# A hybrid decoder layer: three projections in products of 512 columns, and background steps handed out at another pace

## The chip, the cores and the metric

The kernel runs on one core of a Trainium2 chip. The metric is the device time of one execution in microseconds (us), lower is better; the median of three runs stands for the kernel. Beside it there is one profiled execution, whose trace gives every instruction of the engines: TensorE (PE for matmuls, PEld for weight loads), VectorE (DVE), ScalarE (ACT), GpSimd (POOL) and SyncE (SP), and the packets of the DMA queues.

## The reference

One decoder layer over 256 tokens of width 1024, in float32: a SwiGLU feed-forward (FFN), then a mixer of two parallel branches, then a second FFN, each between norms. Only the mixer's first projection and what reads it concern us:

```python
u = rmsnorm(h, mix_pre_g[l])
z, xbc, dt_raw, q, k, v, gate_logits = jnp.split(u @ w_in[l], IN_SPLITS, axis=-1)
y_ssd = ssd_branch(z, xbc, dt_raw, ...)     # chunked state-space scan; y * silu(z), norm, @ w_branch
y_att = diff_attn_branch(q, k, v, ...)      # 8 heads, two softmaxes each, p0 - lam * p1, norm, @ w_branch
gates = jax.nn.sigmoid(gate_logits + gate_b[l]).reshape(b, L, N_BRANCH, D_MODEL)
merged = gates[:, :, 0] * y_ssd + gates[:, :, 1] * y_att
h = h + rmsnorm(merged @ w_out[l], mix_post_g[l])
```

z has 2048 columns, q and k have 1024 each; q is scaled by 1/8 before the scores.

## The kernel before

**Precision and products.** Every float32 matrix is split into a high and a low part in a reduced float format (`F32R`): `hi` is a cast, `lo` is the rest. A product is the sum of three: high weight by high activation, high weight by low activation, low weight by high activation. Activations `u` live in two tiles in which, for each slab of 128 input channels, the 256 high columns and the 256 low columns lie next to each other. `act_u` (L430) hands out the high part, the low part, or both at once as 512 columns.

**Weights.** Weights come by DMA in chunks of 1 MB (`raw`, three buffers, on SP's queue), and each chunk is split into two `whi` tiles by ACT (L249) and two `wlo` tiles by DVE (L252). `take()` (L276) returns the next chunk's parts and first splits as many chunks as three ahead. These tiles are from a pool of 29 buffers of 4 KB a partition (`k4`), which also holds most tiles of the mixer.

**Two ways to make a product of 256 output channels by 256 tokens.** `mm_t` (L293) makes it with 256-column matmuls: for each half of 128 channels 8 slabs by (high weight x high activation, high weight x low activation), then 8 slabs of low weight x high activation, so 48 matmuls, each with its weight load; the high weight is loaded twice. Both halves share one PSUM bank, and one ACT operation moves it to SBUF. `mm_w` (L305) loads the high weight once and multiplies it with both activations in a matmul of 512 columns, and the low weight with the high activation in one of 256: 32 matmuls and weight loads. Each half fills a whole PSUM bank, with the sum in the first 256 columns and the high x low term in the other 256. ACT copies the second part to the destination (L318) and DVE adds the first part to it (L319). Both take banks from a pool of three, `pj` (L79). Before the change `mm_w` serves the FFNs alone, and `mm_t` serves B and C, xs, z, q and k.

**The order of the mixer.** After v come products for B and C, eight for xs (each followed by the causal convolution on DVE), eight for z (L1321 to L1327), then silu on z, four times q and k (L1333 to L1345), then the gates as four `natural` products of 512 channels (L1352, L1384: two weight chunks and two blocks of 128 tokens each, 12 matmuls of 512 columns at a time), then the SSD branch product `pws`, the attention branch product `pwd`, and the output product.

**The background.** Work that is no large product is written as generators and woven in between the products. A generator does a step and yields its declared cost in us. `back.run(us)` (L1293) adds credit and takes steps until the credit is spent; an overshoot is carried as debt, and a step that yields `BREAK` ends the call and keeps what credit is left. The steps, in the order of the queue:

- `ssd_work`, for each of four groups: two steps that transpose xs and multiply it with dt (0.6 each), four blocks E of exponentials (1.4 each), one state product `py` and its sums on DVE (1.6): 8.4 a group. A group also issues two row broadcasts `acb` by DMA on POOL's queue.
- `ssd_norm`, added after z, for each group: xs * silu(z) and its square (1.2), sums and split (1.5), `BREAK`, a matmul `pn` and the inverse root (0.1), the scaling and split into `yh`, `yl` (2.8); two groups are under way at a time.
- `att_work`, added after q and k, for pairs of heads: scores and softmax (2.3 a head), the combination of the two softmaxes (1.3 a head) with the transposes of the pair before, `BREAK`, values and norm (1.8), transpose of the output (0.8).

A call follows each z, q and k product with `BG_US`, each of the 16 gate blocks with `GATE_US`, and each of the 16 `pws` blocks with `SSD_US`.

**Who sets the order.** From the end of the first v products up to line 1350 the framework's planner orders the instructions of every engine by the place in the program and its own estimate of when they are ready. From line 1350, `own_order(PE)`, PE runs its matmuls in the order in which they are written, while the planner goes on ordering the other engines. Every engine executes its list strictly in order.

Of the kernel before, what the change touches and what calls it, by code (L numbers as in the profile page):

```python
# [18 lines left out]
AF = mybir.ActivationFunctionType  # L19
ALU = mybir.AluOpType  # L20
# [7 lines left out]
T = 256  # L28
# [12 lines left out]
WARM = 3  # L41
FILL = 2
TAIL = 3
BG_US = 3.15
GATE_US = 1.35
SSD_US = 1.55
DOWN = {"f1": "p q1 p p q2 p ppp", "f2": "q1 p q2 p q3 ppp"}
FIRST, LAST = (1, 2, 3, 5, 7, 6, 4), (1, 6, 7, 2, 5, 3, 4)
# [4 lines left out]
def tile_hybrid_layer(ctx: ExitStack, tc: tile.TileContext, x, ffn1_pre_g, ffn1_w_gate, ffn1_w_up,  # L53
# [4 lines left out]
    nc = tc.nc  # L58
# [5 lines left out]
    def k4(shape, name, dt=F32):  # L64
        return sb.tile(shape, dt, tag="k4", name=name, bufs=K4_BUFS)
# [13 lines left out]
    def pj(name):  # L79

        return ps.tile([P, 512], F32, tag="pj", name=name, bufs=3)

    def pjt(name):

        return pj(name).rearrange("p (m t) -> p m t", m=2)

    def bg(shape, name):
        return ps.tile(shape, F32, tag="bg", name=name, bufs=5)
# [169 lines left out]
    def split_to(n):  # L258

        while len(splits) < min(n, len(units)):  # L260
            of, p = units[len(splits)]
            if p is not None:
                splits.append(of.split(p))
                continue
            for _ in split_steps():
                pass

    def ahead_of(i, n):

        n *= 4  # L270
        while n > 0 and i < len(units):
            n -= 4 if units[i][1] is None else 1
            i += 1
        return i

    def take(ahead=AHEAD):  # L276

        i = taken[0]
        taken[0] += 1
        split_to(ahead_of(i, ahead))  # L280
        (of, p), w = units[i], splits[i]
        splits[i] = None
        if p is not None:
            return w
        his, los = w
        nj = chunks[of][1][1] // 2
        return (lambda j: his[j // nj][:, j % nj, :], lambda j: los[j // nj][:, j % nj, :])
# [5 lines left out]
    def mm_t(acc, w, act, k0=0, first=True, last=True, ks=range(KD)):  # L293

        (wh, wl), (ah, al, _) = w, act
        acc = acc if isinstance(acc, list) else [acc[:, m, :] for m in range(2)]
        for m in range(2):
            cs = slice(m * P, (m + 1) * P)
            for j in ks:
                nc.tensor.matmul(acc[m], wh(j)[:, cs], ah(k0 + j), start=first and j == ks[0], stop=False)  # L300
                nc.tensor.matmul(acc[m], wh(j)[:, cs], al(k0 + j), start=False, stop=False)  # L301
            for j in ks:
                nc.tensor.matmul(acc[m], wl(j)[:, cs], ah(k0 + j), start=False, stop=last and j == ks[-1])  # L303

    def mm_w(dst, name, w, act):  # L305


        (wh, wl), (ah, _, ahl) = w, act
        for m in range(2):
            acc = pj(f"{name}{m}")  # L310
            cs = slice(m * P, (m + 1) * P)
            for j in range(KD):
                if j:
                    nc.tensor.matmul(acc[:, :T], wl(j)[:, cs], ah(j), start=False, stop=False)  # L314
                nc.tensor.matmul(acc, wh(j)[:, cs], ahl(j), start=j == 0, stop=j == KD - 1)  # L315
                if not j:
                    nc.tensor.matmul(acc[:, :T], wl(j)[:, cs], ah(j), start=False, stop=False)
            nc.scalar.copy(dst[:, m, :], acc[:, T:])  # L318
            nc.vector.tensor_tensor(dst[:, m, :], acc[:, :T], dst[:, m, :], ALU.add)  # L319

    def mm_nat(acc, w, act, k0, first, last, late):

# [26 lines left out]
    def act_table(name):  # L349
        f = nc.scalar.preload_act_table_set(name)  # L350
        for prev in act_since:
            tc.add_manual_dep(f.ins, prev, order, reason="activation table")
        act_since.clear()
        act_fence[0] = f.ins.name
# [71 lines left out]
    def new_u(tag):  # L426
        for i in range(2):
            uT[i] = sb.tile([P, 4, 2, T], F32R, tag="u8", name=f"u{i}_{tag}", bufs=2)

    act_u = (lambda j: uT[j // 4][:, j % 4, 0, :], lambda j: uT[j // 4][:, j % 4, 1, :],  # L430
             lambda j: uT[j // 4][:, j % 4, :, :])
# [294 lines left out]
    def ffn(post_v, tag, ready, turned, then, products):  # L726
# [28 lines left out]
        for j in range(2, FF // T):  # L755
            if j % 2 == 0:
                gh = k4([P, 4, T], f"gh_{tag}{j}", F32R)
                gl = k4([P, 4, T], f"gl_{tag}{j}", F32R)
            o = (j % 2) * 2
            gu += [(gh[:, o + m, :], gl[:, o + m, :]) for m in range(2)]  # L760
            sg = k2([P, 2, T], f"sg_{tag}{j}")
            mm_w(sg, f"pg_{tag}{j}", take(), act_u)
            act(sg, sg, AF.Silu)
            su = k2([P, 2, T], f"su_{tag}{j}")
            mm_w(su, f"pup_{tag}{j}", take(), act_u)
            nc.vector.tensor_tensor(sg, su, sg, ALU.mult)  # L766
            split(gh[:, o:o + 2, :], gl[:, o:o + 2, :], sg)
            if j // 2 in QUADS[tag]:
                if j % 2:
                    sums[j // 2] = sums_of(j // 2, even, sg)  # L770
                else:
                    even = sg
# [253 lines left out]
    for i in range(4):  # L1026
        acc = pjt(f"pbc{i}")
        mm_t(acc, take(), act_u)
        dst = (bT, cT)[i // 2]
# [16 lines left out]
    sz = [None] * 4  # L1046
# [94 lines left out]
    qT = [None] * 2  # L1141
    kT = [None] * 2
# [167 lines left out]
    back = Background()  # L1310
    back.add(cb_work())
    for g in range(4):
        xs[g] = k4([P, 4, T], f"xs{g}")
        for i in range(2):
            acc = pjt(f"pxs{g}{i}")
# [5 lines left out]
    for g in range(4):  # L1321
        sz[g] = k4([P, 4, T], f"sz{g}")
        for i in range(2):
            acc = pjt(f"pz{g}{i}")
            mm_t(acc, take(), act_u)
            nc.scalar.copy(sz[g][:, i * 2:i * 2 + 2, :], acc)
            back.run(BG_US)  # L1327
    act_table(SILU)
    for g in range(4):
# [3 lines left out]
    for c in range(4):  # L1333
        if c % 2 == 0:
            qT[c // 2] = k4([P, 4, T], f"q{c}")
            kT[c // 2] = k4([P, 4, T], f"k{c}")
        o = (c % 2) * 2
        acc = pjt(f"pq{c}")
        mm_t(acc, take(), act_u)
        nc.scalar.activation(qT[c // 2][:, o:o + 2, :], acc, AF.Copy, scale=0.125)  # L1340
        back.run(BG_US)
        acc = pjt(f"pk{c}")
        mm_t(acc, take(), act_u)
        nc.scalar.copy(kT[c // 2][:, o:o + 2, :], acc)
        back.run(BG_US)  # L1345

    back.add(att_work())

# [3 lines left out]
    def natural(name, n, hi, lo, evict, us, then=lambda: None):  # L1352


        accs = [pj(f"{name}{b}") for b in range(2)]
        for i in range(n):
            w = take()
            for b in range(2):
                bs = slice(b * P, (b + 1) * P)
                mm_nat(accs[b], w, (lambda k: hi(k)[:, bs], lambda k: lo(k)[:, bs]), i * 4, i == 0, i == n - 1, "u")  # L1360
                if i == n - 1:
                    evict(b, accs[b])
                back.run(us)
            if i == 0:
                then()
# [9 lines left out]
    for half in range(2):  # L1375
# [4 lines left out]
        for q in range(2):  # L1380
            def gate(b, acc):
                nc.vector.tensor_tensor(gt[half][b][:, halves[q]], acc, gb[:, halves[q]], ALU.add)

            natural(f"pgt{half}{q}", 2, uh, ul, gate, GATE_US)  # L1384
    opens.append(open_gates)
# [42 lines left out]
    acc = [[bg([P, 512], f"acc_mx{b}{q}") for q in range(2)] for b in range(2)]  # L1428
# [47 lines left out]
```

## Time and profile before

| what | us |
|---|---|
| median of three runs (739.06 to 739.86) | 739.17 |
| the profiled execution | 739.06 |
| its span, first to last instruction | 737.4 |

A row such as `L319 DVE TENSOR_TENSOR su_f<-pup_f,su_f 128x256 ... x36 | 15.1, 421 | 26.1 <-ACT` reads: line 319, on DVE, writes tile `su_f` from `pup_f` and `su_f`, on 128 partitions by 256 elements, 36 times; 15.1 us busy, 421 ns each on average; the engine was idle 26.1 us just before them, most of it until an ACT instruction. Buffer numbers are left out of tile names. A row of the timeline gives start, length, engine, line and tiles, with a number of like instructions merged; starts are in us from the beginning of the span. A row of waits reads: who waited, for what, us in total, times, longest. In the rows by stretch each engine has its busy time and in brackets its instructions. A matmul's busy time includes its latency through the array, so successive matmuls overlap, and their pitch is read from starts.

### The profile page before, as it was taken

To read this page: it belongs to the slowest core of one execution; us is meant where nothing else is said; L and a number is where in the kernel's file an instruction comes from. 1 tells how busy PE (TensorE), PEld (TensorE's weight loads), DVE (VectorE), ACT (ScalarE), POOL (GpSimd) and SP (SyncE) were. 2 spreads that over 40 slices of the span, in tenths; PEclk is the share of its full clock that TensorE was granted. 3 is DMA by queue.
4 is the path that set the end of the run, shared out by engine and by line. 5 is a ranking of instruction groups with operands and counts; after the bars stand their busy time and mean duration, and the time that the engine had idled before them with its cause. 6 is when DMAs were issued, how large, how long until landed. Compare 5 with 4: busy or idle time off the path is not lost.

```text
span 737.4 us, 11114 instructions
## 1 busy us (share of the span) xinstructions
PE 728.1 (99%) x4339; PEld 635.0 (86%) x4339; DVE 586.8 (80%) x888; ACT 460.6 (62%) x769; POOL 38.9 (5%) x72
## 2 busy tenths in 40 slices
PE   8999999999999999999999999999999999999996
PEld 6888888888889999999999888888888888888874
DVE  7978768998677888777878997685784878779994
ACT  6657556665566565959957666782563657566562
POOL 2700000000300000000000000000010000000000
PEclk9999999999999999999999999999999999999999
DMA  8884674469353647666556555365371764664541
GB/s 298 228 262 151 216 229 171 160 214 344 117 172 117 207 137 231 195 184 221 169 162 214 171 172 208 134 234 194 120 237 44 229 195 155 222 215 142 189 168 57
DMA packets 94214, 137.97 MB, mean 187 GB/s; under 512 B 2685, under 2 KB 68305, under 8 KB 94161
## 3 DMA queue, kind: packets, MB, share of 16 engines
q1 hardware_dynamic: 91488, 129.51, 53.7%
q0 software_dynamic: 2368, 7.22, 3.2%
q8 instruction: 34, 0.56, 0.3%
q10 hardware_dynamic: 304, 0.53, 0.2%
q14 instruction: 20, 0.16, 0.1%
HBM read 136.17 MB, written 1.08 MB: 186 GB/s over the span
## 4 chain that ended last, share of the span: by engine, by line
PE 96%; DVE 2%; issue 1%; ACT 0%; DMA 0%; DVEq 0%; ACTq 0%
PE pup_f L315 9%; PE pg_f L315 9%; PE pws L330 6%; PE pgt L330 6%; PE acc_f1p L620 5%; PE pg_f L314 4%; PE pup_f L314 4%; PE acc_f2p L620 3%; PE pn_f L330 3%; PE pn_f L340 3%; PE acc_mx L568 3%; PE pn_mx L330 3%; PE pwd L330 3%; PE acc_f1p L568 3%; PE pz L301 2%; PE pxs L303 2%
## 5 line engine op out<-in xcount | busy, mean ns | idle before, releaser
L252 DVE TENSOR_TENSOR wlo<-raw,whi 128x1024 fp32r<-128x1024 f32 (+1 forms) x226 | 266.5, 1209 | 25.3 <-ACT whi L249 22.2
L249 ACT CAST whi<-raw 128x1024 fp32r<-128x1024 f32 (+1 forms) x225 | 225.8, 1043 | 21.2 <-PE pgt L330 5.9
L315 PE MATMUL pg_f<-u_f,whi 128*128 128x512 f32 x288 | 101.3, 396 | 0.0
L315 PE MATMUL pup_f<-u_f,whi 128*128 128x512 f32 x288 | 101.3, 396 | 0.0
L314 PE MATMUL pg_f<-u_f,wlo 128*128 128x256 f32 x252 | 70.6, 280 | 0.0
L314 PE MATMUL pup_f<-u_f,wlo 128*128 128x256 f32 x252 | 70.2, 279 | 0.0
L315 PEld LDWEIGHTS pup_f<-u_f,whi 128*128 128x128 f32 x288 | 52.8, 188 | 9.9 <-issue 0.2
L315 PEld LDWEIGHTS pg_f<-u_f,whi 128*128 128x128 f32 x288 | 52.8, 188 | 9.7
L314 PEld LDWEIGHTS pg_f<-u_f,wlo 128*128 128x128 f32 x252 | 47.5, 188 | 1.7
L314 PEld LDWEIGHTS pup_f<-u_f,wlo 128*128 128x128 f32 x252 | 47.5, 188 | 1.7
L319 DVE TENSOR_TENSOR su_f<-pup_f,su_f 128x256 f32<-128x256 f32 x36 | 15.1, 421 | 26.1 <-ACT su_f L318 26.0
L129 ACT CAST wqh<-wt 128x1024 fp32r<-128x1024 f32 x20 | 21.1, 1053 | 23.5 <-DVE wt L121 17.2
L318 ACT COPY su_f<-pup_f 128x256 f32<-128x256 f32 x36 | 13.4, 372 | 35.1 <-PE pup_f L315 35.0
L330 PE MATMUL pgt<-whi,u_mx 128*128 128x512 f32 x128 | 33.1, 393 | 0.0
L300 PE MATMUL pxs<-u_mx,whi 128*128 128x256 f32 x128 | 31.7, 285 | 0.0
L301 PE MATMUL pz<-u_mx,whi 128*128 128x256 f32 x128 | 31.6, 284 | 0.0
L300 PE MATMUL pz<-u_mx,whi 128*128 128x256 f32 x128 | 31.6, 284 | 0.0
L301 PE MATMUL pxs<-u_mx,whi 128*128 128x256 f32 x128 | 31.4, 283 | 0.0
L330 PEld LDWEIGHTS pgt<-whi,u_mx 128*128 128x128 f32 x128 | 23.6, 188 | 5.4 <-DVE yl L291 0.3
L1004 DVE SCALAR_TENSOR_TENSOR xs<-pxs,cols_b,xs 128x255 f32<-128x255 f32 (+2 forms) x48 | 21.9, 476 | 6.3 <-ACT xs L1001 5.9
L290 ACT CAST gh_f<-sg_f 128x512 fp32r<-128x512 f32 x18 | 11.2, 621 | 21.8 <-DVE sg_f L766 21.8
L301 PEld LDWEIGHTS pz<-u_mx,whi 128*128 128x128 f32 x128 | 24.5, 192 | 0.2 <-issue 0.2
(395 smaller groups left out, 1709.5 us busy)
## 6 DMA issues: line engine op xcount, KB each, us to landing
raw<-in_w_in_dram SPq DMA_DIRECT2D x40, 1024.0 KB, 5.4
raw<-in_ffn_w_down_dram SPq DMA_DIRECT2D x22, 1024.0 KB, 4.9
raw<-in_ffn_w_gate_dram SPq DMA_DIRECT2D x20, 1024.0 KB, 5.6
raw<-in_ffn_w_up_dram SPq DMA_DIRECT2D x20, 1024.0 KB, 5.5
raw<-in_ssd_w_branch_dram SPq DMA_DIRECT2D x8, 1024.0 KB, 5.1
acb<-acd POOLq DMA_DIRECT2D x8, 512.0 KB, 5.2
raw<-in_da_w_branch_dram SPq DMA_DIRECT2D x4, 1024.0 KB, 5.1
raw<-in_w_out_dram SPq DMA_DIRECT2D x4, 1024.0 KB, 5.0
```

What stands on the lines that cost most here:

```text
L129: nc.scalar.copy(hi, src)
L249: copy(hi[:, js, :], r[:, q * nj + j:q * nj + j + n, :])
L252: nc.vector.tensor_sub(lo[:, js, :], r[:, q * nj + j:q * nj + j + n, :], hi[:, js, :].bitcast(F32))
L300: nc.tensor.matmul(acc[m], wh(j)[:, cs], ah(k0 + j), start=first and j == ks[0], stop=False)
L301: nc.tensor.matmul(acc[m], wh(j)[:, cs], al(k0 + j), start=False, stop=False)
L314: nc.tensor.matmul(acc[:, :T], wl(j)[:, cs], ah(j), start=False, stop=False)
L315: nc.tensor.matmul(acc, wh(j)[:, cs], ahl(j), start=j == 0, stop=j == KD - 1)
L330: nc.tensor.matmul(acc, a(k0 + j), b(j), start=first and i == 0, stop=last and i == 11)
L340: nc.tensor.matmul(accs[b], x_(k0 + j), w_(j), start=first and j == 0 and w_ is wh and x_ is acts[b][0], stop=last and j == 3 and w_ is wl)
L568: nc.tensor.matmul(acc[b][q], x_[:, ts], w_(kt)[:, halves[q]], start=begin and i == 0 and kt == 0 and x_ is ah and w_ is wh, stop=i == n - ...
L620: nc.tensor.matmul(bank[p], x_, w_, start=p not in begun, stop=last and p in (1, 5, 6, 7))
L1004: nc.vector.scalar_tensor_tensor(dst[:, m, s:], acc[:, m, :T - s], cw(3 - s, c), dst[:, m, s:], ALU.mult, ALU.add)
```

## The change

z, q and k go through `mm_w` instead of `mm_t`. `mm_w` gets a `scale`, used by q, which is applied by ACT to the second part and by DVE to the first. The paces are new: `BG_US`, now of z alone, 2.7 instead of 3.15; `QK_US` 2.8 after q and k, where 3.15 was used; `GATE_US` 1.75 instead of 1.35. `SSD_US` stays at 1.55.

```diff
-BG_US = 3.15
-GATE_US = 1.35
+BG_US = 2.7
+QK_US = 2.8
+GATE_US = 1.75
 SSD_US = 1.55
...
-    def mm_w(dst, name, w, act):
+    def mm_w(dst, name, w, act, scale=None):
...
-            nc.scalar.copy(dst[:, m, :], acc[:, T:])
-            nc.vector.tensor_tensor(dst[:, m, :], acc[:, :T], dst[:, m, :], ALU.add)
+            if scale is None:
+                nc.scalar.copy(dst[:, m, :], acc[:, T:])
+                nc.vector.tensor_tensor(dst[:, m, :], acc[:, :T], dst[:, m, :], ALU.add)
+            else:
+                nc.scalar.activation(dst[:, m, :], acc[:, T:], AF.Copy, scale=scale)
+                nc.vector.scalar_tensor_tensor(dst[:, m, :], acc[:, :T], scale, dst[:, m, :], ALU.mult, ALU.add)
...
-            acc = pjt(f"pz{g}{i}")
-            mm_t(acc, take(), act_u)
-            nc.scalar.copy(sz[g][:, i * 2:i * 2 + 2, :], acc)
+            mm_w(sz[g][:, i * 2:i * 2 + 2, :], f"pz{g}{i}", take(), act_u)
             back.run(BG_US)
...
-        acc = pjt(f"pq{c}")
-        mm_t(acc, take(), act_u)
-        nc.scalar.activation(qT[c // 2][:, o:o + 2, :], acc, AF.Copy, scale=0.125)
-        back.run(BG_US)
-        acc = pjt(f"pk{c}")
-        mm_t(acc, take(), act_u)
-        nc.scalar.copy(kT[c // 2][:, o:o + 2, :], acc)
-        back.run(BG_US)
+        mm_w(qT[c // 2][:, o:o + 2, :], f"pq{c}", take(), act_u, 0.125)
+        back.run(QK_US)
+        mm_w(kT[c // 2][:, o:o + 2, :], f"pk{c}", take(), act_u)
+        back.run(QK_US)
```

## The prediction

> **What bounds the kernel now.** I read the page first: busy times, the chain that ended last, the costliest groups.
>
> ```profile
> span 737.4 us, 11114 instructions
> PE 728.1 (99%) x4339; PEld 635.0 (86%) x4339; DVE 586.8 (80%) x888; ACT 460.6 (62%) x769; POOL 38.9 (5%) x72
> PE 96%; DVE 2%; issue 1%; ACT 0%; DMA 0%; DVEq 0%; ACTq 0%
> L319 DVE TENSOR_TENSOR su_f<-pup_f,su_f 128x256 f32<-128x256 f32 x36 | 15.1, 421 | 26.1 <-ACT su_f L318 26.0
> L318 ACT COPY su_f<-pup_f 128x256 f32<-128x256 f32 x36 | 13.4, 372 | 35.1 <-PE pup_f L315 35.0
> ```
>
> PE carries 96% of the chain. A busy PE may still be a waiting PE, so the list of PE's waits comes second; it is complete in four rows.
>
> ```profile
> PE warm L406 <- POOL ident L392: 1.6, 1, 1.6
> PE pn_f L340 <- DVE raw_u L459: 0.3, 1, 0.3
> PE pu_f L451 <- DMA h<-in_x_dram: 0.2, 1, 0.2
> PE acc_f2p L568 <- DVE wlo L252: 0.2, 1, 0.2
> ```
>
> None of them lies in the mixer. So in z, q/k and gates the kernel is as long as the stream of matmuls, and only two things can move the end: fewer PE nanoseconds, or another engine becoming late. Third, the stretches: z (289.4 to 344.0), q/k (to 397.2), gates (to 447.2), the SSD branch product (to 502.5), the busiest part of the gates, and all of z to gates together.
>
> ```profile
> 289.40:344.00 54.60, 54.58 (x475) 52.74 (x474) 42.85 (x73) 40.23 (x82) 2.65 (x5) 1.00 0.65 203
> 344.00:397.20 53.20, 53.20 (x462) 51.44 (x461) 42.90 (x62) 41.56 (x68) 1.59 (x3) 1.00 0.57 173
> 397.20:447.20 50.00, 50.00 (x249) 40.86 (x248) 43.86 (x76) 30.64 (x61) 0.53 (x1) 1.00 0.64 214
> 447.20:502.50 55.30, 55.30 (x298) 45.94 (x296) 44.82 (x75) 42.53 (x80) 0.00 (x0) 1.00 0.54 191
> 402.20:442.80 40.60, 40.60 (x200) 32.85 (x199) 36.89 (x67) 24.50 (x52) 0.53 (x1) 1.00 0.55 178
> 289.40:447.20 157.80, 157.78 (x1181) 145.04 (x1180) 129.61 (x209) 112.43 (x209) 4.78 (x9) 1.00 0.62 196
> ```
>
> After the length the columns are PE, PEld, DVE, ACT, POOL, granted clock, DMA. VectorE is the second engine: 82% over z to gates (129.61 of 157.80), 91% for 40 us of the gates, and PE did not wait even there.
>
> **The products (what is removed).** The first matmuls of consecutive products give their pitch. The first three rows are the FFN, which already has the 512-column form; the last two are the first z product, which no background work interrupts.
>
> ```profile
> 42.92 0.39 PE L315 MATMUL pg_f<-u_f,whi 128*128 128x512 f32 x1
> 48.52 0.39 PE L315 MATMUL pup_f<-u_f,whi 128*128 128x512 f32 x1
> 54.11 0.39 PE L315 MATMUL pg_f<-u_f,whi 128*128 128x512 f32 x1
> 289.50 0.28 PE L300 MATMUL pz<-u_mx,whi 128*128 128x256 f32 x1
> 295.26 0.38 PE L1056 MATMUL px<-ident,xs 128*128 128x128 f32 x2
> ```
>
> New form: (54.11 - 42.92) / 2 = 5.595 us. Old form: 295.26 - 289.50 = 5.76 us. Both push the same 12,288 columns; 48 matmuls and weight loads become 32. Gain 0.165 us a product, and 16 products (8 z, 4 q, 4 k): 2.6 us. It lies on the path whole, since PE never waits there. The Trainium skill (TensorE: Matmul & The Clock Gate, "Back-to-back issue gap") counts columns / 2.4 plus 2.5 ns a matmul; that would give 16 x 16 x 2.5 ns = 0.64 us, an estimate from that page and a time of 738.4. The two pitches above show four times that, 0.165 against 0.04 us a product, and they decide.
>
> **The evictions (what is added).** Before, one ACT operation moved both halves of a product:
>
> ```profile
> L1326 ACT COPY sz<-pz x8: 560/586/590, 295.5 to 344.3; 128x512 f32<-128x512 f32 x8
> ```
>
> Now each half has an ACT copy of 128x256 (0.372 us, row L318) and a DVE add that reads PSUM (0.421 us, row L319). ACT: 32 x 0.372 - 16 x 0.586 = 2.5 us more, against 45 us in which it is idle from z to gates: nothing. DVE: 32 x 0.42 = 13.4 us more. The four q products scale in the add, a form this trace lacks for a PSUM operand of that kind; the nearest row is the scaled sum below, 0.476, so 0.42 to 0.48 and at most 0.5 us more in all; I take 0.42, since the read of PSUM is that of L319.
>
> **The pace (what is moved).** Each paced step has a declared cost and a call hands out steps until its credit is spent. Credit to the end of the gates is unchanged: 16 x 3.15 + 16 x 1.35 = 72.0 before, 8 x 2.7 + 8 x 2.8 + 16 x 1.75 = 72.0 after. From there on all lies where it did, save that the first pair's values and norm slip one call, past the gates. Spending the credits by hand: the last E block and the state product of SSD group 2 move from z to q/k; three norm steps of groups 2 and 3 (square, sums, square) move from q/k to the gates; in the gates the attention starts at the seventh call instead of the fifth.
>
> ```profile
> L1078 DVE TENSOR_TENSOR E<-E,cbm 128x768 f32<-128x768 f32 x16 | 15.3, 957 | 7.9 <-ACT E L357 7.9
> L1073 DVE TENSOR_SCALAR E<-acb,acs 128x128 f32<-128x128 f32 x32 | 7.1, 280 | 0.0
> L1095 DVE SCALAR_TENSOR_TENSOR xs<-xs,cols_b,py 128x256 f32<-128x256 f32 x16 | 6.9, 476 | 1.9 <-PE py L1088 1.9
> L1102 DVE TENSOR_TENSOR xs<-xs,sz 128x1024 f32<-128x1024 f32 x4 | 4.8, 1221 | 1.4 <-ACT sz L357 1.4
> L1106 DVE TENSOR_TENSOR sqy<-sqy 128x512 f32<-128x512 f32 x4 | 2.7, 683 | 0.0
> L1107 DVE TENSOR_TENSOR sqy<-sqy 128x256 f32<-128x256 f32 x4 | 1.7, 423 | 0.1
> L291 DVE TENSOR_TENSOR ssum<-sqy,ssum 128x256 fp32r<-128x256 f32 x4 | 1.7, 417 | 0.0
> 289.40:447.20 157.80, 11.28 (x128) 8.01 (x128) 1.00 0.62 196
> acb<-acd POOLq DMA_DIRECT2D x8, 512.0 KB, 5.2
> ```
>
> An E block is (15.3 + 7.1) / 16 = 1.4 us of DVE, a state product's sums 6.9 / 4 = 1.7, and its matmuls 11.28 / 4 = 2.8 us of PE (row before the last: L1088 alone). Three norm steps are 2 x 1.22 + 0.68 + 0.42 + 0.42 = 4.0 us of DVE. The attention pair takes 1.3 us of PE (447.2 less its start at 445.96, quoted below) out of the gates. VectorE's load by stage then:
>
> z: 42.85 + 6.7 - 3.1 = 46.5 in 54.6 - 1.3 - 2.8 = 50.5 us, 92%.
> q/k: 42.90 + 6.7 + 3.1 - 4.0 = 48.7 in 53.2 - 1.3 + 2.8 = 54.7 us, 89%.
> Gates: 43.86 + 4.0 = 47.9 in 50.0 - 1.3 = 48.7 us, 98%.
> Together 143.0 in 153.9, 93%, so it still fits, narrowly; the branch product behind it has 55.3 - 44.8 = 10.5 us free on DVE, into which lag can run off.
>
> No load of weights is issued elsewhere. The moved steps bring no DMA but the row-sum broadcasts of SSD group 3 on POOL's queue, whose engine is 5% busy; they start later together with the E blocks that need them, so I cost them at nothing; if one landed late, its E block would be late by a landing, 5.2 us in the fence above, and the group's state product behind it. Norm tiles of groups 2 and 3 stay three calls longer (a call is 50.0 / 16 = 3.1 us) in the shared pool of 4 KB tiles, so the gates' weight splits find fewer free ones. That is not in the sum; it belongs to the slower rival.
>
> **The wait that is new.** The DVE add waits for its ACT copy; queued behind it on DVE are weight low parts and background steps, and PE waits for the add through PSUM: three banks, now one a half product instead of one a product. From the end of a half, PE has two halves (5.6 us, plus what background lies between) before it needs the bank again, where it had two products. How late evictions can be is seen here:
>
> ```profile
> 56.69 0.40 PE L315 MATMUL pg_f<-u_f,whi 128*128 128x512 f32 x1
> 61.12 0.74 DVE L319 TENSOR_TENSOR sg_f<-pg_f,sg_f 128x256 f32<-128x256 f32 x2
> 364.22 1.12 PE L303 MATMUL pq<-u_mx,wlo 128*128 128x256 f32 x8
> 368.30 0.58 ACT L1340 ACTIVATE q<-pq 128x512 f32<-128x512 f32 x1
> ```
>
> In the FFN an add ended 4.4 us after its half (56.69 + 0.40 to 61.12 + 0.42) and PE did not wait. In q/k, ACT itself came 3.0 us after the product (365.34 to 368.30). The two together, 3.0 + 4.4 + 0.4 = 7.8, would exceed 5.6 by 2.2 us, less some background. Bounds for stalls of this kind: none, and two such coincidences, 4.4 us. I take 0.5 us, nearer to none, because of 72 FFN halves the same three banks stalled no PE, and z and q/k have about 1 us of background matmuls a product that stretches the allowance.
>
> **The sum.** Profiled execution 739.06 (span 737.4 and 1.7 around it), 0.1 under the median of 739.17. 739.06 - 2.6 + 0.5 = 736.96; with the 0.1 to the median, about 737.0.
>
> **The rivals.** *A. No change.* One or two late evictions, 2.2 us each at most, eat the gain: 739.1 - 2.6 + 2.2 = 738.7. For it: ACT is full for stretches in z and q/k; against it: the FFN.
> *C. Columns alone set the pace.* Old and new form push the same columns; if loads and instruction counts were free, the gain would be nil and the time 739.1. Only the two pitches speak, 5.76 against 5.595, and they speak against it. The Trainium skill's count above comes nearest to this case.
>
> *B. Slower: VectorE becomes the bound in the gates.* VectorE's idle time from z to gates:
>
> ```profile
> DVE E L1078 <- ACT E L357: 7.9, 13, 1.7
> DVE wlo L252 <- ACT whi L249: 7.2, 6, 2.0
> DVE yl L291 <- ACT yh L290: 5.1, 4, 1.7
> 392.45 2.46 DVE L252 TENSOR_TENSOR wlo<-raw,whi 128x1024 fp32r<-128x1024 f32 x2
> 398.29 0.39 PE L330 MATMUL pgt<-wlo,u_mx 128*128 128x512 f32 x1
> 445.96 0.39 PE L1208 MATMUL po<-v,aT 128*128 128x128 f32 x2
> ```
>
> Of the 28.2 us idle (157.80 - 129.61), the second row is an engine ahead of its work and can vanish; if the other 21.0 all stay, being hand-overs with nothing to fill them, DVE needs 143.0 + 21.0 = 164.0 us. PE offers 153.9, and the shortest lead of the weights, at the first gate product, is 3.4 us (398.29 - 394.91). Stall 164.0 - 157.3 = 6.7: 739.1 - 2.6 + 6.7 = 743.2. It decides once more than 157.3 - 143.0 = 14.3 us stay forced, and costs the whole gain at 16.9. For it: 98% in the gates, PE there in written order, so that a late norm or softmax stops all behind it. Against it: a loaded engine has other work queued in those gaps, and 402.2 to 442.8 shows 91% with no PE wait.
>
> **How the numbers follow.** A run of this kernel tells about 0.2%, 1.5 us, from no change; the gain of 2.6 passes that if stalls stay under 1.1. Forecast 0.57, A 0.15, C 0.03, B 0.25; A and C are the 0.18 of no change. The likeliest alone spans 736.0 (no stall, and 0.5 us less from fewer breaks in the stream) to 737.7. With A, C and most of B the range is 735.8 to 743.0; B's end beyond that is about 1 in 10. Faster 0.57, same 0.18, slower 0.25.
>
> **What would show it.** The pitch of an uninterrupted z product 5.60 instead of 5.76, else the first term is wrong. DVE adds of 0.42 on sz, q and k, 32 of them. z to gates shorter by 2.6 and 1.3 us, with DVE near 143 us busy. No row of PE waiting for DVE or ACT in the mixer over 0.5 us; a row of z, q or k behind an eviction means A, rows in the gates behind weights, norms or softmax mean B.

## The result, and the profile after

The changed kernel takes 743.16 us (median of six runs, 742.79 to 744.02) against 739.23 before in the same series: 1.0052 of it, interval 1.0042 to 1.0063. It is slower by 3.9 us, where 2.2 us faster was forecast. The profiled execution took 743.29 with a span of 741.6.

First three lines from the page of the changed kernel, then the longest of the six rows in its list of PE's waits; the other five are of 0.2 to 1.6 us and lie outside the stages from z to the branch product. Its line numbers are up to five above those of before: L316 is the matmul of 512 columns in `mm_w`, L320/L321 its copy and add, L323/L324 the scaled pair for q.

```profile
span 741.6 us, 10624 instructions
PE 728.1 (98%) x4083; PEld 622.3 (84%) x4083; DVE 597.5 (81%) x920; ACT 462.3 (62%) x785; POOL 38.8 (5%) x72
PEclk9999999999999999999899999999999999999999
```

```profile
PE pk L316 <- DVE q L324: 4.0, 1, 4.0
```

This row is new: PE stood once, for 4.0 us, before a matmul of a k product, until a DVE add of q was done. And the line of the granted clock has an 8 where all of before was 9. The same by stretch: z, q/k, gates and branch product, cut at the first matmul of each.

```profile
289.37:342.81 53.44, 53.44 (x347) 45.57 (x345) 45.48 (x82) 38.26 (x82) 2.63 (x5) 1.00 0.68 208
342.81:401.42 58.61, 54.60 (x333) 45.69 (x332) 47.94 (x77) 41.80 (x79) 1.59 (x3) 0.94 0.59 187
401.42:450.19 48.77, 48.77 (x236) 39.44 (x235) 45.77 (x81) 33.35 (x66) 0.53 (x1) 1.00 0.51 162
450.19:506.66 56.47, 56.47 (x308) 47.32 (x306) 45.48 (x77) 43.07 (x81) 0.00 (x0) 1.00 0.59 200
289.37:506.66 217.29, 213.28 (x1219) 178.03 (x1217) 184.68 (x315) 156.47 (x305) 4.74 (x9) 0.98 0.60 190
```

Against before, z is 1.2 us shorter (54.60), q/k 5.4 longer (53.20), the gates 1.2 shorter and the branch product 1.2 longer (the attention pair that slipped over the border). The whole loss lies in q/k. The last row, from the first z matmul to the first matmul of the attention branch product, is the measure used below; before it is 502.49 - 289.50 = 212.99 us. How the wait comes about stands in ACT's timeline of the changed kernel, with rows of PE and DVE around the wait:

```profile
346.20 1.28 ACT L355 ACT_TABLE_LOAD   x1
347.50 3.91 ACT L362 ACTIVATE sz<-sz 128x1024 f32<-128x1024 f32 x4
351.41 1.28 ACT L355 ACT_TABLE_LOAD   x1
352.70 1.04 ACT L250 CAST whi<-raw 128x1024 fp32r<-128x1024 f32 x1
353.66 0.40 ACT L362 ACTIVATE E<-acb,acs 128x128 f32<-128x128 f32 x1
353.96 0.64 ACT L323 ACTIVATE q<-pq 128x256 f32<-128x256 f32 x2
```

```profile
342.81 0.39 PE L316 MATMUL pq<-u_mx,whi 128*128 128x512 f32 x1
348.40 0.39 PE L316 MATMUL pk<-u_mx,whi 128*128 128x512 f32 x1
350.99 0.40 PE L316 MATMUL pk<-u_mx,whi 128*128 128x512 f32 x1
353.78 1.23 DVE L253 TENSOR_TENSOR wlo<-raw,whi 128x1024 fp32r<-128x1024 f32 x1 [2.83 <-ACT whi L250]
354.93 0.75 DVE L324 SCALAR_TENSOR_TENSOR q<-pq,q 128x256 f32<-128x256 f32 x2
355.40 0.80 PE L316 MATMUL pk<-u_mx,whi 128*128 128x512 f32 x1 [4.01 <-DVE q L324]
357.03 4.34 PE L1093 MATMUL py<-E,X 128*64 128x256 f32 x32
```

The four silus of z with a table load on either side hold ACT from 346.20 to 352.69, and a weight cast and an exponential follow. The two halves of the first q product, done on PE by 348.6, are copied out from 353.96, and their adds start at 354.93, behind a weight split on DVE. With one bank a half, q's halves hold two of the three banks and the first half of k the third; its second half finds none until 355.4. Then the clock, in stretches of the wait, of the time right behind it and after that:

```profile
351.00:355.40 4.40, 0.39 (x4) 0.07 (x2) 1.62 (x3) 4.38 (x10) 0.00 (x0) 0.76 0.13 49
355.40:360.10 4.70, 4.70 (x24) 3.17 (x26) 4.09 (x6) 2.73 (x5) 0.00 (x0) 0.50 0.77 227
360.10:366.00 5.90, 5.90 (x46) 5.00 (x43) 4.66 (x9) 2.28 (x4) 0.53 (x1) 1.00 0.94 263
```

After the wait PE worked for 4.7 us at a granted clock of 0.50, which by that clock loses half, 2.35 us. (In the row of the wait the clock is 0.76: the slow spell began within the wait, where it costs nothing.) Wait and half clock make 6.4 us; the measured 4.3 in the stretch (217.29 - 212.99) leaves 2.1 us that the new products do give.

### The profile page after: what moved, and what is told of

It reads as the page before. It is cut to its first block, busy times and chain, and to the rows that moved or that the text cites. A ratio compares the mean times of both kernels' runs of the same rounds, so it can differ in the third digit from the quotient of the medians.

```text
span 741.6 us, 10624 instructions
## 1 busy us (share of the span) xinstructions
PE 728.1 (98%) x4083; PEld 622.3 (84%) x4083; DVE 597.5 (81%) x920; ACT 462.3 (62%) x785; POOL 38.8 (5%) x72
## 4 chain that ended last, share of the span: by engine, by line
PE 93%; DVE 3%; ACT 2%; issue 1%; DMA 0%; DVEq 0%; ACTq 0%
PE pup_f L316 9%; PE pg_f L316 9%; PE pws L335 6%; PE pgt L335 6%; PE acc_f1p L625 5%; PE pz L316 4%; PE pg_f L315 4%; PE pup_f L315 4%; PE pn_mx L335 3%; PE pn_f L335 3%; PE acc_mx L573 3%; PE pn_f L345 3%; PE pwd L335 3%; PE acc_f1p L573 3%; PE acc_f2p L625 2%; PE pxs L304 2%
## 5 line engine op out<-in xcount | busy, mean ns | idle before, releaser
L316 PE MATMUL pup_f<-u_f,whi 128*128 128x512 f32 x288 | 101.3, 396 | 0.0
L316 PE MATMUL pg_f<-u_f,whi 128*128 128x512 f32 x288 | 101.3, 396 | 0.0
L316 PEld LDWEIGHTS pup_f<-u_f,whi 128*128 128x128 f32 x288 | 52.8, 188 | 9.9
L316 PEld LDWEIGHTS pg_f<-u_f,whi 128*128 128x128 f32 x288 | 52.8, 188 | 9.7
L316 PE MATMUL pz<-u_mx,whi 128*128 128x512 f32 x128 | 45.1, 400 | 0.0
L321 DVE TENSOR_TENSOR su_f<-pup_f,su_f 128x256 f32<-128x256 f32 x36 | 15.1, 420 | 25.6 <-ACT su_f L320 25.5
L320 ACT COPY su_f<-pup_f 128x256 f32<-128x256 f32 x36 | 13.4, 373 | 34.6 <-PE pup_f L316 34.5
L315 PE MATMUL pz<-u_mx,wlo 128*128 128x256 f32 x112 | 31.4, 280 | 0.0
L316 PEld LDWEIGHTS pz<-u_mx,whi 128*128 128x128 f32 x128 | 23.4, 188 | 4.7 <-DVE sz L321 0.2
L316 PE MATMUL pk<-u_mx,whi 128*128 128x512 f32 x64 | 23.3, 406 | 4.0 <-DVE q L324 4.0
```

## The experiments

The theory: one wait of 4.0 us for a PSUM bank behind the silu block, half clock after it, and otherwise a gain as forecast. Rival "pace": the steps moved into the gates overload VectorE. Rival "products": adds and banks cost more than the matmuls give, everywhere. Each kernel was timed against the kernel before on the same chip, whose median was 739.16 (first four), 739.76 (next four) and 739.53 (last two); the changed kernel stands with its own series, where that median was 739.23. The column "stretch" goes from the first z matmul to the first matmul of the attention branch product in the profiled execution.

| kernel | us | ratio to before, interval | stretch, us | PE's waits in it, us |
|---|---|---|---|---|
| before | 739.23 | 1 | 212.99 | none |
| changed | 743.16 | 1.0052, 1.0042 to 1.0063 | 217.29 | 4.0 |
| e1_old_pace | 738.07 | 0.9985, 0.9976 to 0.9994 | 211.71 | 0.4, 0.3 |
| e2_old_products | 739.59 | 1.0010, 1.0001 to 1.0019 | 213.33 | none over 0.2 |
| e3_q_before_silu | 738.91 | 0.9994, 0.9985 to 1.0003 | 212.63 | 1.6 |
| e4_fill_wait | 741.42 | 1.0030, 1.0019 to 1.0042 | 214.99 | none |
| e5_q0_old | 738.65 | 0.9988, 0.9977 to 1.0000 | 212.83 | 1.0, 0.3 |
| e6_z_pace_old | 738.52 | 0.9983, 0.9968 to 0.9997 | 212.44 | 1.0, 0.4 |
| e7_qk_only | 744.35 | 1.0060, 1.0038 to 1.0082 | 217.76 | 3.6, 0.5 |
| e8_pace_more_qk | 738.35 | 0.9981, 0.9967 to 0.9995 | 211.61 | 0.4, 0.2 |
| e9_pace_3_0 | 740.56 | 1.0013, 1.0004 to 1.0022 | 214.27 | 0.9, 0.8, 0.5, 0.3 |
| e10_pace_2_9 | 742.22 | 1.0032, 1.0020 to 1.0044 | 216.68 | 2.3, 0.6, 0.5 |

**The new products with the old paces.**

```diff
-BG_US = 2.7
-QK_US = 2.8
-GATE_US = 1.75
+BG_US = 3.15
+QK_US = 3.15
+GATE_US = 1.35
```

> The products of 512 columns with the old paces (3.15, 3.15, 1.35). Theory (one wait of 4.0 us for a PSUM bank behind the silu block on ACT, then half clock, and else the gain as forecast): with the old pace the state product of group 2 and a transpose, 3.5 us of PE work, come between the halves of the first q product and the second half of the first k product, so the bank is free in time or nearly: no wait over 1 us, no half clock, 739.2 - 2.6 + 0 to 1 = 736.6 to 737.6. Rival pace (VectorE overloaded in the gates by the moved steps): also about 736.6, with DVE below 90% in the gates. Rival products (the 32 added DVE adds and the banks held a half each cost more than the matmuls give, everywhere): 743 as with the change.

738.07, faster than before. PE and ACT of this kernel around the silu block:

```profile
343.82 0.39 PE L316 MATMUL pq<-u_mx,whi 128*128 128x512 f32 x1
346.74 2.82 PE L1093 MATMUL py<-E,X 128*64 128x256 f32 x32
352.38 1.03 PE L1061 MATMUL px<-ident,xs 128*128 128x128 f32 x8
355.81 0.62 PE L316 MATMUL pk<-u_mx,whi 128*128 128x512 f32 x2
353.94 0.64 ACT L323 ACTIVATE q<-pq 128x256 f32<-128x256 f32 x2
355.40 0.75 DVE L324 SCALAR_TENSOR_TENSOR q<-pq,q 128x256 f32<-128x256 f32 x2
```

ACT reaches q 10.1 us after the first q matmul (353.94 - 343.82), where it took 11.2 in the changed kernel, and the first add ends 9.0 us after its half instead of 9.6. But PE has the state product (2.8 us) and a transpose (0.8) to do between, and gets to the second half of k at about 356.0 (the second matmul of the fourth row). The first add, from 355.40 and 0.42 us long, had freed the bank about 0.2 us before. The wait is not on the list. So the old pace makes the delay a little shorter and covers the rest, with little to spare; it does not remove it. The time is 0.5 us over the forecast; the stretch shows two short waits for that (0.4 and 0.3 us) and a gain that is smaller than 2.6.

**The old products with the new paces.** The kernel before, with 2.7, 2.8 and 1.75.

> The old products of 256 columns with the new paces (2.7, 2.8, 1.75). Theory: one bank a product, so the silu block delays nobody; 739.2, within 0.7. Rival pace: the moved steps load the gates as before, 742 to 743. Rival products: 739.2.

739.59, 0.1% over before and far from 742. Pace alone costs next to nothing; the rival "pace" falls. Only with the new products does the pace matter, as it decides what covers the wait.

**Silus behind the first q product.**

```diff
-    act_table(SILU)
-    for g in range(4):
-        act(sz[g], sz[g], AF.Silu)
-    act_table(EXP_LN)
-    back.add(ssd_norm(range(4)))
...
         mm_w(qT[c // 2][:, o:o + 2, :], f"pq{c}", take(), act_u, 0.125)
+        if c == 0:
+            open_z()
         back.run(QK_US)
```

`open_z` holds the lines taken out.

> The changed kernel, with the silu block of z written after the first q product instead of before it, so that ACT moves both halves of q out before the four silus. Theory: no wait at the first k product, clock 1.00 throughout, 739.2 - 2.6 = 736.6, up to 737.5. Rival pace and rival products: 743, since neither paces nor products differ from the changed kernel.

738.91: 4.3 us better than the changed kernel by moving one block, with products and paces as they are, so the rival "products" falls too. It missed its forecast by 1.4 us. A wait of 1.6 us stands in its list, 20 us behind the silus:

```profile
348.92 0.66 ACT L323 ACTIVATE q<-pq 128x256 f32<-128x256 f32 x2
349.46 3.90 ACT L362 ACTIVATE sz<-sz 128x1024 f32<-128x1024 f32 x4
368.84 1.26 ACT L362 ACTIVATE E<-acb,acs 128x128 f32<-128x128 f32 x4
371.47 0.63 ACT L320 COPY k<-pk 128x256 f32<-128x256 f32 x2
373.64 0.76 DVE L321 TENSOR_TENSOR k<-pk,k 128x256 f32<-128x256 f32 x2
374.12 0.50 PE L316 MATMUL pq<-u_mx,whi 128*128 128x512 f32 x1 [1.57 <-DVE k L321]
```

Now q leaves before the silus (348.92). The first k product leaves late (358.71), but nobody waits for it. The half that waits is the second of the third q product, for a bank of the second k product: ACT copied that one at 371.47, after a run of E blocks and a weight cast, and DVE added it at 373.64. So another irregular block, the E blocks, delays the evictions here; whether it would without the silus' new place is not shown. The clock did not drop there.

**The wait filled with work.**

```diff
             acc = pj(f"{name}{m}")
+            if name == "pk0" and m == 0:
+                for j in range(18):
+                    nc.tensor.matmul(acc, wh(j % KD)[:, cs], ahl(j % KD), start=True, stop=True)
```

> The changed kernel with 18 more matmuls of 512 columns ahead of the first half of the first k product, into its own bank, which the product then starts anew; 18 x 0.227 = 4.1 us of PE work that nobody reads. Theory: they take up the wait of 4.0 us, and because PE does not stand idle the clock stays at full speed, which saves the 2.4 us that half clock cost: 743.2 - 2.4 = 740.8. If the wait costs 4.0 us but the half clock nothing: 743.2. If the place is not where the time goes: 743.2 + 4.1 = 747.3.

Its stretch, whole:

```profile
290.07:505.06 214.99, 214.99 (x1237) 180.14 (x1235) 184.25 (x315) 156.54 (x305) 4.75 (x9) 1.00 0.59 192
```

With 4.1 us more work (18 matmuls from 349.12, the product's own first matmul at 353.21) the stretch is 2.3 us shorter than in the changed kernel (217.29), at full clock and with PE busy throughout. That is the price of the half clock, 2.35 by the row above. The timed gain is 1.7 us, 0.6 less than forecast. Between the two profiled executions it is 1.4: the one with the filled wait reached z 0.7 us later, and up to there the kernels run the same work. The run also gives the net worth of the new products: 214.99 - 4.1 - 212.99 = -2.1 us.

**The first q product alone in the old form**, the rest of the changed kernel as it is.

> The changed kernel with the first q product alone in the old form (one bank for both halves, 48 matmuls), new paces. Theory: the four silus hold back one bank instead of two, the next need of it is a product later, so the wait of 4.0 us goes, the clock stays full; what is left of the gain is 15/16 of 2.05, the net gain that the filled run shows: 739.2 - 1.9 = 737.3, up to 737.9 with a short wait for that bank. If the wait belongs to the new form in general or to the paces: 743.

738.65; the 4.0 us and the half clock are gone, by a change to one product of sixteen. It is 0.75 us over the end of its forecast, which had the kernel before at 739.2 and not at 739.76. Two waits remain: 0.3 us for the bank of the first q product, still behind the silus, and 1.0 us at 373.56, for a bank of the second k product behind the E blocks, the same place as in the kernel with the silus behind the first q product.

**The pace after z alone.** 3.15 after z, 2.8 after q and k, 1.525 in the gates.

> All products in the new form; the pace after z as before (3.15), after q and k as changed (2.8), gates 1.525, again 72 of credit in all. Theory: the pace after z alone decides whether the state product of group 2 stands between the two halves of the first q product, which covers the wait; so no long wait: 739.2 - 2.05 = 737.1, up to 738.1 with short waits as in the run with the old paces. If the paces of q, k or the gates made the wait: 741 to 743.

738.52, 0.4 over the forecast, with no wait at the first k product; it is the z pace that decides. Of its two waits the longer is for the sums of the norm in the gates.

**q and k in the new form, z in the old one.**

```diff
-            mm_w(sz[g][:, i * 2:i * 2 + 2, :], f"pz{g}{i}", take(), act_u)
+            acc = pjt(f"pz{g}{i}")
+            mm_t(acc, take(), act_u)
+            nc.scalar.copy(sz[g][:, i * 2:i * 2 + 2, :], acc)
```

> New paces, q and k in the new form, z in the old one. Theory: z's own evictions have no part in the wait, which needs only the silu block and q and k with a bank a half; so the wait of about 4 us and the half clock stay, and half of the net gain is missing: 743.2 + 1.0 = 744.2, within 0.8. If z's added DVE work delays the silus and so makes the wait: under 741.

744.35, as expected, with the wait and the half clock:

```profile
PE pk L316 <- DVE q L324: 3.6, 1, 3.6
357.30:360.70 3.40, 2.85 (x18) 1.70 (x18) 3.40 (x4) 2.05 (x3) 0.00 (x0) 0.50 0.96 295
```

z's added work on DVE has no part in it beyond a few tenths (3.6 against 4.0).

**More of the norm ahead of the gates**: 3.15, 3.3 and 1.275.

> All products in the new form; paces 3.15 after z, 3.3 after q and k, 1.275 in the gates, 72 of credit in all, so that the norm steps are given out earlier than with the old paces. Theory: no wait at the first k product, and none for the sums of the norm at the gates (0.3 us in the run with the old paces): 737.1 to 737.8. If VectorE's load in q and k decides (42.9 before, some 50 here): waits there, 739 or more.

738.35, with the shortest stretch of all (211.61), but 0.55 over the forecast: the wait for the norm's sums is 0.2 us and not gone, and the one profiled execution, 739.13, waits 1.1 us more ahead of z. Its DVE load of q/k, 47.98 us in a stretch of 52.05, made no wait there.

**Two paces between.** 3.0, 3.3, 1.35; and 2.9, 3.3, 1.4.

> All products in the new form; paces 3.0 after z, 3.3 after q and k, 1.35 in the gates, 72 of credit in all. Spending the credit, the last E block and the state product of group 2 are still given out by the last z call (24.0 of credit against 23.6 needed), ahead of the silus. Theory: no wait at the first k product and fewer short waits in z than with 3.15: 737.1 to 738.0, the net gain of 2.05 less at most 0.9.

> The same with 2.9 after z and 1.4 in the gates (72 in all but 0.2). Now the last z call still gives out the last E block, but the state product falls behind the silus in the written order. If what matters is that E block (it must be through ACT before the silus, so that its state product can run while the bank is held): no wait over 1 us and no half clock, 737.1 to 738.1. If it is the written place of the state product, or a load on VectorE that grows as z gets less and q and k more: a wait near 4 us and half clock, 742 to 743.

The first missed its forecast: it waits 0.9 us at the first k product, and 1.6 more behind it (a state product waits for its E block, the norm's sums are late in the gates). The second waits 2.3 us at the first k product and gets half clock for one spell:

```profile
347.73 1.28 ACT L355 ACT_TABLE_LOAD   x1
349.88 2.82 PE L1093 MATMUL py<-E,X 128*64 128x256 f32 x32
355.18 0.64 ACT L323 ACTIVATE q<-pq 128x256 f32<-128x256 f32 x2
357.42 0.50 PE L316 MATMUL pk<-u_mx,whi 128*128 128x512 f32 x1 [2.30 <-DVE q L324]
357.80:361.10 3.30, 3.30 (x12) 2.84 (x11) 3.30 (x5) 0.18 (x1) 0.00 (x0) 0.50 0.88 263
```

Having the last E block ahead of the silus is not enough: it stands on ACT before them, so the block of silus begins 1.5 us later (347.73 instead of 346.20) and q leaves later by 1.2. The state product does run in between (349.88), as in the kernel with the old paces; but the first add of q ends 11.6 us after its half, where 9.0 were covered there (10.3 in the run with 3.0). The first alternative of that expectation is refuted. The time and the half clock are those of the second, but its reasons do not hold: the state product was in place, and what differs is the start of the silus, 4.9 us after the first q matmul instead of 1.7. With all z, q and k in the new form the wait at the first k product was 0, 0.9, 2.3 and 4.0 us for paces of 3.15, 3.0, 2.9 and 2.7 after z.

## Why the prediction was wrong

*The products.* The mechanism was right, the size too large. An uninterrupted product takes 348.40 - 342.81 = 5.59 us, as forecast, but the net gain is 2.1 us, not 2.6. The pitch had been taken where no background work breaks the stream. Behind such a break the first matmul costs more, in the changed kernel (first two rows) and in the kernel before (last two):

```profile
333.47 0.50 PE L316 MATMUL pz<-u_mx,whi 128*128 128x512 f32 x1
333.81 0.28 PE L318 MATMUL pz<-u_mx,wlo 128*128 128x256 f32 x1
350.54 0.39 PE L300 MATMUL pq<-u_mx,whi 128*128 128x256 f32 x1
350.76 0.28 PE L301 MATMUL pq<-u_mx,whi 128*128 128x256 f32 x1
```

That is 0.34 us to the next start, against 0.23 inside a product, and 0.22 against 0.12: about 0.1 us more in either form. Summed over the matmuls next to breaks in z, q and k, it is some 1.1 us in the kernel before and 1.35 in the one with the filled wait (an estimate from the two traces). So breaks explain about half of the missing 0.5 us at most; the rest stays open. One uninterrupted product stood for all sixteen.

*The evictions.* Right as costs: 32 adds of 0.42 us, the scaled ones at 0.417 no dearer, and ACT's part came to 2.4 us more; no run shows a price for it apart from the waits.

*The pace.* The sums of the credit were right, the places only in the written order: in both kernels the planner ran the state product of group 2 after the first q matmuls or later, so z did not become shorter by 2.8 us. That VectorE fits was right: 45.77 of 48.77 us in the gates, 94% busy, and no PE wait in that stage. Rival B has nothing behind it in this kernel; its mechanism shows small in the other paces, as 0.2 to 1.0 us for the norm's sums.

*The wait that is new.* This step failed: "The two together, 3.0 + 4.4 + 0.4 = 7.8, would exceed 5.6 by 2.2 us" and the 0.5 us taken from it. The queue, the banks and the allowance were named correctly; the lateness was not. It took 3.0 us from one q product as ACT's worst, and did not look at what stands on ACT ahead of the very first one, though the trace of before shows it:

```profile
347.79 2.82 PE L1088 MATMUL py<-E,X 128*64 128x256 f32 x32
346.60 1.28 ACT L350 ACT_TABLE_LOAD   x1
347.89 3.90 ACT L357 ACTIVATE sz<-sz 128x1024 f32<-128x1024 f32 x4
351.80 1.28 ACT L350 ACT_TABLE_LOAD   x1
353.09 1.05 ACT L249 CAST whi<-raw 128x1024 fp32r<-128x1024 f32 x1
354.05 0.59 ACT L1340 ACTIVATE q<-pq 128x512 f32<-128x512 f32 x1
```

This block of 6.5 us was already there and q was copied at the same time, 354.05. It harmed nobody, because the copy was due only when the whole product was done at 353.0, with the state product inside it. In the new form the first half was due at 345.8 and its add ended at 355.3, 9.6 us late instead of 7.8: ACT came 8.2 us after the half and not 3.0, and the add ended 1.4 us after that and not 4.8. The allowance was the bare 5.6 us of two halves, with no background in it: the state product, inside the first q product before (347.79), now came after the wait (357.03). The difference of 9.6 and 5.6 is the wait of 4.0. Rival A had the right mechanism, and a price of 2.2 us for it.

*What no step had.* That PE standing idle for 4.0 us costs more than 4.0 us. The sum treated a stall as its own length; the half clock added 2.35. Without it the time would have been about 740.8, still slower than before.

*The remark that the first pair's values slip out of the gates* was right (1.2 us from one stage to the next) and worth nothing in the end.

The version with the new products and the paces 3.15, 3.15 and 1.35 is faster than both kernels, by 0.15% against before (1.1 us), as is 3.15, 3.3 and 1.275 by 0.19% (1.4 us). That is less than the 2.1 us that the products give; about 0.6 us of it goes to short waits.

## What to carry to other kernels

When a change makes a buffer smaller or due sooner, look at the next use of it after every irregular block on the engine that empties it (a table switch, a run of long activations), not at a typical use: the block need not be new or longer to start to hurt. Background work between two products is also cover for late evictions, so a pace is to be judged by what it leaves uncovered and not by its sum. A stall on PE as long as those here (2.3 us and more) is to be priced with the slow clock behind it. When one long wait is gone, the list of waits is to be read again: here the E blocks stood next in line.

## What was unexpected of the hardware

How short a wait can bring the half clock. Waits of 4.0, 3.6 and 2.3 us each brought a spell at a granted clock of 0.50; a wait of 1.6 us did not:

```profile
372.00:374.10 2.10, 0.55 (x3) 0.19 (x2) 2.10 (x4) 2.10 (x7) 0.00 (x0) 1.00 0.00 0
374.10:378.00 3.90, 3.88 (x36) 2.99 (x38) 3.90 (x6) 3.74 (x5) 0.00 (x0) 1.00 0.82 253
```

These rows are the kernel with the silus behind the first q product, around and after its wait. The Trainium skill (TensorE: Matmul & The Clock Gate, "Why this matters for your kernels") advises against PE idle gaps over about 3 us. The 2.3 us of the kernel with pace 2.9 lie below that and were enough, so here the measurement decides; where between 1.6 and 2.3 us it begins, and whether it depends on when the wait falls, these runs do not tell.
